# Start offsets of split fp32 operands in a one-core transformer stack: from 64- or 128-byte offsets to 1024-byte ones

## The chip, the cores and the metric

The program runs on one core of a Trainium2 chip, in one launch. The metric is the device time of that launch in microseconds. Three runs of the kernel before took 2493.84, 2503.16 and 2496.09 us; the median is 2496.09 us.

## The reference, cut to what matters

The model works on 256 tokens of width 1024 in float32. A first block has a mixer (gated delta rule and mLSTM side by side), a gated feed-forward part of 22 x 128 hidden units and a small gated embedding. A second block has a linear recurrence (RG-LRU), a PEER layer, forgetting attention, and another PEER layer. A PEER layer scores 16,384 experts per token through 8 heads with 2 x 128 sub-keys and combines the 16 best of each head:

```python
h = _rmsnorm(x, g_ffn)
x = x + (jax.nn.silu(h @ w1) * (h @ w3)) @ w2
...
q = (xc @ q_w).reshape(TOKEN_CHUNK, PEER_HEADS, 2, PEER_HALF)
u = jnp.take(expert_u, expert, axis=0)
act = jax.nn.gelu(jnp.einsum('thkd,td->thk', u, xc).astype(jnp.float32), approximate=False)
w = (g * act).astype(xc.dtype)
return jnp.einsum('thk,thkd->td', w, jnp.take(expert_v, expert, axis=0))
```

Nearly all of the arithmetic is products of a 256-token activation with a weight of 1024 rows or columns. The kernel computes both PEER products densely, over all 16,384 experts, and multiplies by a gate that is zero for the experts that were not chosen.

## The kernel before, in words

**Split products.** Every large float32 product is made of three passes in the type fp32r. An operand x is split into `hi` (x rounded to fp32r, a ScalarE copy) and `lo` (x minus hi, on VectorE or GpSimd); the product is hi*hi + hi*lo + lo*hi, all summed in one PSUM bank (`mm3`; its matmuls carry line L323).

**Weights** come as 766 blocks of 128 x 1024 floats (512 KB) through one queue of loads on SyncE, in the order of use (`Stream`). Each block passes through three tiles: `raw` (4 buffers, L202), `whi` (2 buffers, cast at L209) and `wlo` (2 buffers, subtracted at L257 on VectorE or L259 on GpSimd). `sub_pattern` says block by block which of the two engines subtracts.

**Activations** stand feature-major in SBUF: `hh` and `hl` are the two halves of the normalized activation, [128 partitions, 8 slices of features, 256 tokens], so a slice is 1024 bytes in each partition. Other split operands have their own tiles: `oab` (both mixer outputs), `fh`/`fl` (the feed-forward's hidden slice), `p` (the embedding), `xbh`/`xbl` (the recurrence), `rawh`/`rawl` (the activation before its norm is known: the product is made on unscaled rows and scaled after, `norm`, `set_raw` and `linear`; with a shift column these rows hold 258 values, 1032 bytes).

**Which operand moves.** A matmul loads a 128 x 128 stationary operand (a weight load, PEld in the profile) and streams the moving one through it. In `block`/`mm3` (L323) and `kblock` (L1051) the weights are stationary and 256 tokens move: 256 columns, 1024 bytes. In `tblock` (L1065, the PEER v stage), and in `alin` and attention's values, 128 tokens are stationary and 512 columns of `whi` or `wlo` move: 2048 bytes.

**Stages on the time line**: mixer 0 to 262 us, feed-forward to 459, embedding to 490, recurrence to 652, PEER queries and selection to 800, PEER u to 1126, PEER v to 1482 (its last 8 blocks by `kblock`), attention to 1652, and the second PEER layer to the end (u from about 1800, v from 2137). In the u stage, eight tokens at a time, VectorE builds one-hot tiles `ohB`, `ohE` and `ohA` in 16-bit types (L1583 to L1591) and TensorE multiplies them to the gate `G` (L1600), between the weight blocks.

**Where tiles lie.** The allocator gives each tile the next free multiple of 32 bytes in a partition; 16384 bytes at the bottom are reserved as a DMA scratch. With this the built kernel before has these starts, as bytes past a multiple of 1024:

| tile | role | before |
|---|---|---|
| hh, hl | moving (L323, L1051); stationary (L1065) | 128 |
| whi, wlo | stationary (L323, L1051); moving (L1065) | 448 |
| oab, p | moving (L323) | 448 |
| fh, fl | moving (L1051) | 768 |
| xbh, xbl; rawh, rawl of the embedding | moving | 704 |
| rawh, rawl of 258 columns | moving | 448 to 600, each slice 8 bytes on from the last |
| ohB, ohA | stationary and moving of G | 448 |
| raw | written by the load | 448 |

Of the kernel before, what the change touches and what calls it, by code (L numbers as in the profile page):

```python
# [8 lines left out]
F32 = mybir.dt.float32  # L9
FR = mybir.dt.float32r  # L10
BF = mybir.dt.bfloat16
# [6 lines left out]
P = 128  # L18
# [4 lines left out]
NR = 11  # L23
EPS = 1e-6
BIG = 1e30
TB = 8
TAIL = 8
NLATE = 3
# [153 lines left out]
class Stream:  # L182
# [16 lines left out]
    def _ahead(self, b, n, loads, his, los):  # L199
        while self.nl < min(n, loads) or self.nh < min(n, his) or self.ns < min(n, los):  # L200
            if self.nl < min(n, loads) and self.nl < self.ns + b.raw_bufs:
                t = b.spool.tile([P, D], F32, name="raw", tag="raw", bufs=b.raw_bufs)[:, :self.width(self.nl)]  # L202
                self.load = b.nc.sync.dma_start(t, self.seq[self.nl])
                self.raw[self.nl] = t
                self.nl += 1
                continue
            if self.nh < min(n, his) and self.nh < self.nl:
                t = b.spool.tile([P, D], FR, name="whi", tag="whi", bufs=b.hi_bufs)[:, :self.width(self.nh)]
                b.nc.scalar.copy(t, self.raw[self.nh])  # L209
                self.hi[self.nh] = t  # L210
                self.nh += 1
                continue
            if self.ns < self.nh:
                i = self.ns
                t = b.spool.tile([P, D], FR, name="wlo", tag="wlo", bufs=b.lo_bufs)[:, :self.width(i)]
                b.sub(t, self.raw.pop(i), self.hi[i].bitcast(F32), i)
                self.lo[i] = t
                self.ns += 1
                continue
            raise AssertionError  # L220
# [9 lines left out]
class Build:  # L230
# [121 lines left out]
    def setup(self):  # L352
        nc, pp, d = self.nc, self.pp, self.d
        self.xT = pp.tile([P, KC, S], F32, name="xT")
        self.hh = pp.tile([P, KC, S], FR, name="hh")
        self.hl = pp.tile([P, KC, S], FR, name="hl")
        with self.tc.high_priority(offset=5000):
            for k in range(0, KC, 2):
                nc.sync.dma_start(self.xT[:, k:k + 2], d["xT"][:, k:k + 2])
        self.cst = pp.tile([P, N_PERSIST, P], F32, name="cst")  # L360
        self.cols = pp.tile([P, N_COLS], F32, name="cols")
        nc.scalar.dma_start(self.cols, d["cols"])
        nc.scalar.dma_start(self.cst, d["const"][:, :N_PERSIST])
        self.ident = self.cst[:, C_ID]
        self.ones = self.cst[:, C_ONE]
        self.mhalf = pp.tile([P, 1], F32, name="mhalf")
        nc.vector.memset(self.mhalf, -0.5)
        self.lam = self.colr("lam")
        self.mods = [pp.tile([P, 24], F32, name=f"mod{i}") for i in range(4)]
        self.gsc = [pp.tile([P, KC], F32, name=f"gsc{i}") for i in range(4)]  # L370

        order = []

        def add(k, lo=0, hi=None):
            n = d[k].shape[0]
            order.extend(d[k][i] for i in range(lo, n if hi is None else hi))

        add("w_in")
        add("w_ba")
        add("w_bb")  # L380
        add("w_out")
        for j in range(NFF):
            add("w1", j, j + 1)
            add("w3", j, j + 1)
            if j:
                add("w2", j - 1, j)
        add("w2", NFF - 1, NFF)
        add("w_ple")
        add("w_pg")
        for j in range(NR + GLAG):  # L390
            if j < NR:
                add("l_in", j, j + 1)
            if j >= GLAG:
                i = j - GLAG
                order.append(d["l_gate"][i][:, :2 * len(PAIRS[i]) * P])
        add("l_in", NR, 2 * NR)
        add("l_out")
        for l in (0, 1):
            if l:
                add("f_in")  # L400
                add("f_out")
            add(f"q{l}")
            add(f"u{l}")
            add(f"v{l}")
        self.ws = Stream(self, order)
# [83 lines left out]
                                            op0=OP.mult, op1=OP.subtract)  # L489

    def raw_tiles(self, pool, wide=True):
        w = S + 2 if wide else S
        return (pool.tile([P, KC, w], FR, name="rawh"), pool.tile([P, KC, w], FR, name="rawl"),
                pool.tile([P, S], F32, name="rawb"),
                lambda: (pool.tile([P, S], F32, name="rawt", bufs=2), pool.tile([P, 1], F32, name="rawc", bufs=2)))

# [78 lines left out]
    def mix(self, mp, scr):  # L575
# [2 lines left out]
        gab = mp.tile([P, 16, S], F32, name="gab")  # L578
        gz = mp.tile([P, H, S], F32, name="gz")
        mo = mp.tile([P, H, S], F32, name="mo")  # L580
        oab = mp.tile([P, 16, S], FR, name="oab")
        self.oab = [oab[:, 4 * i:4 * i + 4] for i in range(4)]
        self.norm(scr, self.colr("g_mix"), raw=(
            oab[:, 0:8], oab[:, 8:16], gab[:, 0], lambda: (gab[:, 1 + self.nraw % 2], None)))
# [487 lines left out]
    def ffn(self, fp, scr, fin):  # L1072
# [7 lines left out]
        for j in range(NFF + 1):  # L1080
            if j < NFF:
                p1 = self.linear(self.mmt())
                p3 = self.linear(self.aux("p3"))
                s = fp.tile([P, S], F32, name="fs", bufs=2)
                nc.scalar.activation(s, p1, AF.Silu)
                nc.vector.tensor_tensor(s, s, p3, op=OP.mult)
                h = fp.tile([P, S], FR, name="fh", bufs=3)
                l = fp.tile([P, S], FR, name="fl", bufs=3)
                self.split(h, l, s)
                hm[j] = (h, l)  # L1090
            if j:
# [2 lines left out]
            if j == 8:  # L1094
                pT = fin.tile([P, 2, S], F32, name="pT")
                nc.scalar.dma_start(pT, self.d["pT"])
                self.p_split = [fin.tile([P, 2, S], FR, name=f"p{i}") for i in range(2)]
                for k in range(2):
                    self.split(self.p_split[0][:, k], self.p_split[1][:, k], pT[:, k])
        for n in range(KC):  # L1100
# [76 lines left out]
    def lru(self, fin, scr):  # L1177
        nc = self.nc
        with ExitStack() as es:
            lp = es.enter_context(self.tc.tile_pool(name="lru", bufs=1))  # L1180
            xb = lp.tile([P, NR, S], F32, name="xb")
            xh = lp.tile([P, NR, S], FR, name="xbh")
            xl = lp.tile([P, NR, S], FR, name="xbl")
            hs = lp.tile([P, NR, S], F32, name="hs")
            lam = self.lam
            self.phase("lru")
# [237 lines left out]
    def peer(self, l):  # L1424
# [4 lines left out]
        with ExitStack() as es:  # L1429
# [4 lines left out]
            def region(kb, size):  # L1434
# [3 lines left out]
            es1 = es.enter_context(ExitStack())  # L1438
            rp = es1.enter_context(self.tc.tile_pool(name="raw", bufs=1))
            self.phase(f"peer{l}")  # L1440
            self.norm(big[:, 112:128], self.gsc[mi], self.mods[mi][:, 0:8], raw=(
                rp.tile([P, KC, S + 2], FR, name="rawh"), rp.tile([P, KC, S + 2], FR, name="rawl"), big[:, 0],
                lambda: (big[:, 1 + self.nraw % 2], flat[:, 3 * S + self.nraw:3 * S + self.nraw + 1])))
            qT = region(0, 4096).rearrange("p (a b) -> p a b", a=16)
            sk = region(16, 2048).rearrange("p (a b) -> p a b", a=16)
# [125 lines left out]
            def spread():  # L1571
# [8 lines left out]

                for t0 in range(0, S, TB):
                    tq = slice(t0, t0 + TB)
                    B = op.tile([P, H, P, 2], BF, name="ohB", bufs=2)  # L1583
                    nc.vector.tensor_tensor(B, iop, pairs(items[:, 1, tq]), op=OP.is_equal)
                    nc.vector.tensor_tensor(B, B, pairs(items[:, 2, tq]), op=OP.mult)
                    yield
                    E = op.tile([P, H, P, 2], HF, name="ohE", bufs=1)
                    nc.vector.tensor_tensor(E, iop, pairs(items[:, 0, tq]), op=OP.is_equal)
                    A = op.tile([P, 2, H, P, 2], HF, name="ohA", bufs=2)
                    for i in range(2):  # L1590
                        nc.vector.tensor_tensor(A[:, i], E, pairs(sig[:, i, tq]), op=OP.mult)  # L1591
                    yield
# [148 lines left out]
```

## Time and profile before

| | |
|---|---|
| profiled execution | 2497.24 us |
| its span, first to last instruction | 2495.4 us |
| median of three runs | 2496.09 us |
| TensorE busy | 2380.4 us, 95%, 17450 matmuls |
| weight loads | 2226.6 us, 89% |
| VectorE busy | 1923.4 us, 77% |
| ScalarE busy | 1256.8 us, 50% |
| GpSimd busy | 716.1 us, 29% |
| mean granted TensorE clock | 0.985 |
| data moved | 460 MB, mean 184 GB/s |

A reader should know three things of this profile. The matmuls are pipelined and their ends are modelled: a row's duration (say 1.11 us for 8 matmuls) is longer than the distance to the next row, so the cost of one matmul is read from the distance between the starts of consecutive rows, divided by the count. TensorE works at one of two levels, 1.2 and 2.4 GHz; a granted clock of 1.00 is the upper one. And a VectorE instruction that is held up by GpSimd counts as busy while it is held up.

### The profile page before, as it was taken

The page shows a single profiled execution, that of the slowest core. Times are in us where ns is not written, and L with a number is a line of the kernel's source. Part 1 is how long each engine was busy: PE and PEld are TensorE (multiplying, and loading weights), DVE is VectorE, ACT ScalarE, POOL GpSimd, SP SyncE. Part 2 cuts the span into 40 slices and gives each one's busy share as a digit, 9 for nine tenths or more (in the row PEclk, how much of TensorE's full clock was granted, in tenths as well). Part 3 has the DMA queues.
Part 4 walks back from the last instruction along what each step waited for, and adds up shares of the span by engine and source line. Part 5 has one row for each costly group of instructions (what it writes and reads, how often), then busy time and mean ns, then how long its engine had stood idle before and what let it go on. Part 6 is the DMA issues. An engine that isn't in the chain of part 4 may idle for free. (4 is left out here: it accounts for less than half of the span.)

```text
span 2495.4 us, 44808 instructions
## 1 busy us (share of the span) xinstructions
PE 2380.4 (95%) x17450; PEld 2226.6 (89%) x17450; DVE 1923.4 (77%) x3481; ACT 1256.8 (50%) x2229; POOL 716.1 (29%) x361
## 2 busy tenths in 40 slices
PE   8989999987998999999999998899799999999999
PEld 8989999887998999997888898789799999888888
DVE  7585866889598999986666668878979998655555
ACT  7644544665553444445444556555344444444444
POOL 4635300355666323330000026246522222000000
PEclk9999999989998999999999999999899999999999
DMA  5475677434554555557777755555455555566654
GB/s 192 154 242 190 208 250 251 165 115 137 168 170 139 166 169 161 171 166 245 238 237 244 223 173 192 203 176 161 127 170 161 173 167 169 186 194 191 190 193 152
DMA packets 127252, 460.26 MB, mean 184 GB/s; under 512 B 14128, under 2 KB 14784, under 8 KB 126784
## 3 DMA queue, kind: packets, MB, share of 16 engines
q1 hardware_dynamic: 126000, 454.55, 56.2%
q8 instruction: 136, 2.23, 0.4%
q10 hardware_dynamic: 1040, 2.86, 0.3%
q14 instruction: 76, 0.62, 0.1%
HBM read 456.29 MB, written 1.05 MB: 183 GB/s over the span
## 5 line engine op out<-in xcount | busy, mean ns | idle before, releaser
L209 ACT CAST whi<-raw 128x1024 fp32r<-128x1024 f32 (+1 forms) x766 | 800.8, 1046 | 1000.5 <-PE acc L1065 325.9
L257 DVE TENSOR_TENSOR wlo<-raw,whi 128x1024 fp32r<-128x1024 f32 (+1 forms) x551 | 694.2, 1260 | 378.9 <-ACT whi L209 363.9
L259 POOL TENSOR_TENSOR wlo<-raw,whi 128x1024 fp32r<-128x1024 f32 (+2 forms) x215 | 566.7, 2641 | 754.0 <-ACT whi L209 440.4
L1065 PE MATMUL acc<-whi,hh 128*128 128x512 f32 x960 | 260.5, 392 | 2.6 <-ACT whi L209 1.1
L323 PE MATMUL mm<-hh,whi 128*128 128x256 f32 x1704 | 247.5, 286 | 15.7 <-ACT whi L209 6.6
L1065 PE MATMUL acc<-whi,hl 128*128 128x512 f32 x960 | 259.4, 391 | 0.0
L1065 PE MATMUL acc<-wlo,hh 128*128 128x512 f32 x960 | 259.1, 392 | 0.0
L323 PE MATMUL mm<-hh,wlo 128*128 128x256 f32 x1704 | 245.1, 286 | 13.6 <-DVE wlo L257 11.2
L323 PE MATMUL mm<-hl,whi 128*128 128x256 f32 x1704 | 246.1, 284 | 5.8 <-POOL hl L531 2.9
L323 PEld LDWEIGHTS mm<-hh,whi 128*128 128x128 f32 x1704 | 219.6, 191 | 20.1 <-ACT whi L209 7.8
L323 PEld LDWEIGHTS mm<-hh,wlo 128*128 128x128 f32 x1704 | 219.6, 192 | 16.2 <-DVE wlo L257 12.4
L323 PEld LDWEIGHTS mm<-hl,whi 128*128 128x128 f32 x1704 | 220.5, 192 | 8.3 <-POOL hl L531 4.0
L323 PE MATMUL acc<-hh,wlo 128*128 128x256 f32 x1464 | 207.6, 286 | 14.8 <-DVE wlo L257 12.0
L1065 PEld LDWEIGHTS acc<-whi,hh 128*128 128x128 f32 x960 | 180.1, 188 | 43.1 <-ACT whi L209 1.6
L1065 PEld LDWEIGHTS acc<-whi,hl 128*128 128x128 f32 x960 | 180.3, 188 | 39.8
L1065 PEld LDWEIGHTS acc<-wlo,hh 128*128 128x128 f32 x960 | 180.3, 188 | 39.3
L323 PE MATMUL acc<-hh,whi 128*128 128x256 f32 x1464 | 210.0, 286 | 0.1
L323 PE MATMUL acc<-hl,whi 128*128 128x256 f32 x1464 | 204.6, 281 | 0.0
L323 PEld LDWEIGHTS acc<-hh,wlo 128*128 128x128 f32 x1464 | 189.9, 194 | 15.8 <-DVE wlo L257 12.6
L323 PEld LDWEIGHTS acc<-hh,whi 128*128 128x128 f32 x1464 | 187.4, 192 | 0.3 <-ACT whi L209 0.3
L323 PEld LDWEIGHTS acc<-hl,whi 128*128 128x128 f32 x1464 | 186.4, 190 | 0.0
L422 DVE SCALAR_TENSOR_TENSOR modw<-modw,cb 128x1024 f32<-128x1024 f32 x96 | 130.7, 1366 | 21.5 <-DMA modw<-in_mod_dram 15.2
(523 smaller groups left out, 3304.1 us busy)
## 6 DMA issues: line engine op xcount, KB each, us to landing
raw<-in_u_dram SPq DMA_DIRECT2D x256, 512.0 KB, 3.7
raw<-in_v_dram SPq DMA_DIRECT2D x256, 512.0 KB, 4.1
modw<-in_mod_dram SPq DMA_DIRECT2D x96, 512.0 KB, 4.7
raw<-in_w_dram SPq DMA_DIRECT2D x66, 512.0 KB, 4.3
raw<-in_w_in_dram SPq DMA_DIRECT2D x45, 512.0 KB, 4.2
raw<-in_f_in_dram SPq DMA_DIRECT2D x33, 512.0 KB, 3.6
raw<-in_q_dram SPq DMA_DIRECT2D x32, 512.0 KB, 3.6
raw<-in_l_in_dram SPq DMA_DIRECT2D x22, 512.0 KB, 3.5
```

The source lines that it names most:

```text
L209: b.nc.scalar.copy(t, self.raw[self.nh])
L257: self.anchor = self.nc.vector.tensor_tensor(out, a, b, op=OP.subtract)
L259: self.nc.gpsimd.tensor_tensor(out, a, b, op=OP.subtract)
L323: self.last_mm = mm(ps, t[a], t[b], start=(i == 0), stop=(i == n - 1))
L422: self.later(nc.vector.scalar_tensor_tensor(t, t, 1.0, cb, op0=OP.mult, op1=OP.mult, accum_out=self.mods[i][:, j:j + 1]))
L1065: self.last_mm = mm(accs[h][tb], x[:, tb * P:(tb + 1) * P], w[:, h * 512:(h + 1) * 512], start=(first and i == 0), stop=(last and i == 2))
```

## The change

Every tile that is an operand of a split product gets a start at a multiple of 1024 bytes: `raw`, `whi`, `wlo`, `hh`, `hl`, `oab`, `fh`, `fl`, `p`, `xbh`, `xbl`, `rawh`, `rawl`. The 258-column rows of `rawh`/`rawl` are laid 288 floats (1152 bytes) apart where they were 258 floats (1032 bytes) apart. The three one-hot tiles start at multiples of 256 bytes. The DMA scratch at the bottom of SBUF shrinks from 16384 to 1024 bytes, which makes room for the gaps.

```diff
+ROW = 1024
+RAWW = 288
...
-                t = b.spool.tile([P, D], F32, name="raw", tag="raw", bufs=b.raw_bufs)[:, :self.width(self.nl)]
+                t = b.spool.tile([P, D], F32, name="raw", tag="raw", align_bytes=ROW, bufs=b.raw_bufs)[:, :self.width(self.nl)]
...
-                t = b.spool.tile([P, D], FR, name="whi", tag="whi", bufs=b.hi_bufs)[:, :self.width(self.nh)]
+                t = b.spool.tile([P, D], FR, name="whi", tag="whi", align_bytes=ROW, bufs=b.hi_bufs)[:, :self.width(self.nh)]
...
-                t = b.spool.tile([P, D], FR, name="wlo", tag="wlo", bufs=b.lo_bufs)[:, :self.width(i)]
+                t = b.spool.tile([P, D], FR, name="wlo", tag="wlo", align_bytes=ROW, bufs=b.lo_bufs)[:, :self.width(i)]
...
-        self.hh = pp.tile([P, KC, S], FR, name="hh")
-        self.hl = pp.tile([P, KC, S], FR, name="hl")
+        self.hh = pp.tile([P, KC, S], FR, name="hh", align_bytes=ROW)
+        self.hl = pp.tile([P, KC, S], FR, name="hl", align_bytes=ROW)
...
-        w = S + 2 if wide else S
-        return (pool.tile([P, KC, w], FR, name="rawh"), pool.tile([P, KC, w], FR, name="rawl"),
+        w, n = (RAWW, S + 2) if wide else (S, S)
+        h, l = (pool.tile([P, KC, w], FR, name=k, align_bytes=ROW)[:, :, :n] for k in ("rawh", "rawl"))
+        return (h, l,
...
-        oab = mp.tile([P, 16, S], FR, name="oab")
+        oab = mp.tile([P, 16, S], FR, name="oab", align_bytes=ROW)
...
-                h = fp.tile([P, S], FR, name="fh", bufs=3)
-                l = fp.tile([P, S], FR, name="fl", bufs=3)
+                h = fp.tile([P, S], FR, name="fh", bufs=3, align_bytes=ROW)
+                l = fp.tile([P, S], FR, name="fl", bufs=3, align_bytes=ROW)
...
-            xh = lp.tile([P, NR, S], FR, name="xbh")
-            xl = lp.tile([P, NR, S], FR, name="xbl")
+            xh = lp.tile([P, NR, S], FR, name="xbh", align_bytes=ROW)
+            xl = lp.tile([P, NR, S], FR, name="xbl", align_bytes=ROW)
...
-                    B = op.tile([P, H, P, 2], BF, name="ohB", bufs=2)
+                    B = op.tile([P, H, P, 2], BF, name="ohB", bufs=2, align_bytes=256)
...
-    nc = _bacc.Bacc("TRN2", target_bir_lowering=False, num_devices=1)
+    nc = _bacc.Bacc("TRN2", target_bir_lowering=False, num_devices=1, dynamic_dma_scratch_size=1024)
```

No instruction is moved, added or removed: built, the two kernels have the same instructions in the same order on all five engines, each waiting on the same semaphores. Only addresses differ. In the changed kernel `hh`, `hl`, `whi`, `wlo`, `raw`, `oab`, `p`, `fh`, `fl`, `xbh`, `xbl` and the 256-column `rawh`/`rawl` all start at 0 past a multiple of 1024; slice k of a 258-column row starts at 128 x k past one; a 128-column weight slice starts at 0 or 512; `ohB` starts at 512 and `ohA` at 768. Tiles that the change does not name (`xT`, `scr`, `big`, `gab`, `cst` and the rest) lie 2 to 15 KB lower, at other offsets of 32 bytes.

## Rows read from the trace of the kernel before

**Rows 1.** The page's first parts: engines, and the span in 40 slices.
```profile
span 2495.4 us, 44808 instructions
PE 2380.4 (95%) x17450; PEld 2226.6 (89%) x17450; DVE 1923.4 (77%) x3481; ACT 1256.8 (50%) x2229; POOL 716.1 (29%) x361
...
PEclk9999999989998999999999999999899999999999
```
**Rows 2.** Busy time by stage: engine busy us (instructions), granted clock, DMA share, GB/s.
```profile
0.00:290.00 290.00, 265.11 (x2123) 258.54 (x2124) 212.61 (x356) 168.21 (x296) 146.54 (x85) 0.98 0.56 194
290.00:445.00 155.00, 155.00 (x1318) 155.00 (x1317) 98.14 (x129) 70.37 (x92) 0.00 (x0) 1.00 0.74 249
445.00:655.00 210.00, 181.45 (x1400) 175.81 (x1399) 172.51 (x252) 128.19 (x243) 110.53 (x80) 0.93 0.43 144
655.00:800.00 145.00, 130.01 (x1059) 127.83 (x1058) 129.23 (x476) 70.51 (x118) 93.84 (x37) 0.96 0.46 147
800.00:1130.00 330.00, 328.08 (x3008) 324.63 (x3008) 306.08 (x452) 146.35 (x306) 104.74 (x34) 1.00 0.53 169
1130.00:1482.00 352.00, 350.85 (x1637) 291.75 (x1636) 229.17 (x316) 176.12 (x262) 7.78 (x5) 1.00 0.72 231
1482.00:1665.00 183.00, 166.31 (x1250) 152.51 (x1250) 145.72 (x322) 109.47 (x246) 82.06 (x50) 0.99 0.57 191
1665.00:1800.00 135.00, 115.92 (x957) 114.41 (x957) 121.52 (x457) 65.98 (x107) 79.77 (x36) 0.95 0.45 141
1800.00:2137.00 337.00, 334.64 (x3069) 332.48 (x3068) 304.33 (x456) 149.43 (x312) 90.84 (x37) 0.99 0.53 168
2137.00:2490.00 353.00, 352.77 (x1645) 293.56 (x1645) 201.93 (x267) 172.18 (x256) 0.00 (x0) 1.00 0.59 185
```
**Rows 3.** PE in order of time, feed-forward: start us, us, what, count.
```profile
300.03 1.11 PE L1051 MATMUL acc<-fh,whi 128*128 128x256 f32 x8
...
304.74 1.10 PE L323 MATMUL mm<-hh,wlo 128*128 128x256 f32 x8
```
**Rows 4.** PE in order of time, mixer.
```profile
55.12 1.07 PE L323 MATMUL mm<-hh,wlo 128*128 128x256 f32 x8
...
58.75 1.07 PE L323 MATMUL acc<-hh,whi 128*128 128x256 f32 x8
```
**Rows 5.** PE in order of time, recurrence's output product.
```profile
641.52 1.12 PE L1051 MATMUL acc<-xbh,wlo 128*128 128x256 f32 x8
...
644.40 1.12 PE L1051 MATMUL acc<-xbh,wlo 128*128 128x256 f32 x8
```
**Rows 6.** PE in order of time, attention's products on 258 columns.
```profile
1493.95 1.12 PE L323 MATMUL mm<-rawl,whi 128*128 128x258 f32 x8
1494.91 1.15 PE L323 MATMUL acc<-rawh,whi 128*128 128x258 f32 x8
1495.90 1.12 PE L323 MATMUL acc<-rawl,whi 128*128 128x258 f32 x8
```
**Rows 7.** PE in order of time, PEER v.
```profile
1200.26 1.08 PE L1065 MATMUL acc<-whi,hh 128*128 128x512 f32 x4
...
1203.01 1.08 PE L1065 MATMUL acc<-whi,hh 128*128 128x512 f32 x4
```
**Rows 8.** PE in order of time, mLSTM: plain fp32 products, two records each.
```profile
117.49 0.59 PE L1021 MATMUL mnum<-scr,mv 128*128 128x256 f32 x2
117.92 0.38 PE L1022 MATMUL mnum<-scr,mv 128*128 128x128 f32 x2
```
**Rows 9.** PE in order of time, last blocks of PEER v.
```profile
1458.94 0.62 PE L1051 MATMUL aux<-hh,whi 128*128 128x256 f32 x4
...
1462.11 0.62 PE L1051 MATMUL mm<-hl,whi 128*128 128x256 f32 x4
```
**Rows 10.** The one-hot line L1585 on VectorE: durations ns, min/median/max.
```profile
L1585 DVE TENSOR_TENSOR ohB<-ohB,items x64: 674/679/2903, 787.8 to 2100.8; 128x1024 bf16<-128x1024 bf16 x64
```
**Rows 11.** Chain that ended last, by piece: start us, us, what.
```profile
2137.39 329.19 PE acc L1065 x1437
```

More of the change, by code (lines that the diff above doesn't have):

```diff
@@ L1096, in ffn @@
                 nc.scalar.dma_start(pT, self.d["pT"])
-                self.p_split = [fin.tile([P, 2, S], FR, name=f"p{i}") for i in range(2)]
+                self.p_split = [fin.tile([P, 2, S], FR, name=f"p{i}", align_bytes=ROW) for i in range(2)]
                 for k in range(2):
@@ L1440, in peer @@
             self.phase(f"peer{l}")
+            rh, rl = (rp.tile([P, KC, RAWW], FR, name=n, align_bytes=ROW)[:, :, :S + 2] for n in ("rawh", "rawl"))
             self.norm(big[:, 112:128], self.gsc[mi], self.mods[mi][:, 0:8], raw=(
-                rp.tile([P, KC, S + 2], FR, name="rawh"), rp.tile([P, KC, S + 2], FR, name="rawl"), big[:, 0],
+                rh, rl, big[:, 0],
                 lambda: (big[:, 1 + self.nraw % 2], flat[:, 3 * S + self.nraw:3 * S + self.nraw + 1])))
@@ L1586, in spread @@
                     yield
-                    E = op.tile([P, H, P, 2], HF, name="ohE", bufs=1)
+                    E = op.tile([P, H, P, 2], HF, name="ohE", bufs=1, align_bytes=256)
                     nc.vector.tensor_tensor(E, iop, pairs(items[:, 0, tq]), op=OP.is_equal)
-                    A = op.tile([P, 2, H, P, 2], HF, name="ohA", bufs=2)
+                    A = op.tile([P, 2, H, P, 2], HF, name="ohA", bufs=2, align_bytes=256)
                     for i in range(2):
```

## The prediction

> **What bounds the kernel now.** I read the page's first parts first, then the busy time by stage, then single rows of TensorE in order of time. The reader is to see that TensorE is busy for 95% of the span and that its granted clock is near 1 in nearly all slices [rows 1], the upper level, 2.4 GHz, so the time is the number of matmuls times the cost of one, plus the stretches where something else is waited for. The stages divide it [rows 2]. Five of them have TensorE busy for over 99%: feed-forward (155 us), u (330 and 337 us), v (352 and 353 us), together 1527 us. In the other five (963 us) it is busy for 859, and chains of the mixers, the recurrence, the selection and attention end last in between. The chain that ended last is one unbroken run of 1437 wide matmuls [rows 11]: nothing but their own rate sets the second v stage.
>
> So the change, which moves no instruction and alters only start offsets, can act only through the rate of one instruction, and that rate is worth looking at. Distances between starts, divided by the count, give for 256 columns: 4.71 us for 40 matmuls, 117.8 ns, with moving operands 768 and 128 bytes past a multiple of 1024 [rows 3]; 3.63 us for 32, 113.4 ns, with 128 past [rows 4]; 2.88 us for 24, 120.0 ns, with 704 past [rows 5]. For 258 columns at scattered offsets two sets of eight take 1.95 us, 121.9 ns each [rows 6]. For 512 columns at 448 past it is 2.75 us for 12, 229.2 ns [rows 7]. At 2.4 GHz one column per cycle would be 106.7 and 213.3 ns. A bound from a row: a plain fp32 product streams 256 columns in two records 0.43 us apart, 215 ns each [rows 8], which is 512 cycles and little more. It takes two cycles a column, so it asks for bytes at half the rate, and at that rate an offset of 448 costs nothing that shows. The split products pay 6% to 12% over their columns, and the amount goes with the offset: 704 and 448 are 64 past a multiple of 128, and 768 and 128 are not.
>
> A reading that fits: at full rate the moving stream is fetched in lines of 128 bytes, 32 columns, 13.3 ns each. A row of 1024 bytes that begins 64 past touches nine lines: 120.0 ns, as measured. One of 1032 bytes touches nine wherever it begins: 121.9. One of 2048 bytes that begins 64 past touches seventeen: 226.7 of the 229.2. A row on a line boundary touches eight: 106.7, and the 113.4 or 117.8 measured leave 7 to 11 ns for something else. Two things could be it that the change also touches: the weight slices, which begin 64 past a line and so touch five lines for four, and the row's crossing of a multiple of 1024.
>
> **The change part by part.** *Stationary and moving operands at 1024.* The trace has no matmul at full rate with both operands on a boundary, so the cost is bounded from both sides. Below: 107.5 ns for 256 columns and 215 for 512 (half of, and all of, the fp32 row [rows 8]). Above: each keeps the worst that 256 columns show, 120.0 [rows 5], and 512 columns grow by 6.6 ns, the step between 113.4 and 120.0, to 235.8. I take 110 and 218, near the low end, since 1024-byte rows then touch the fewest lines and cross nothing, but not at it, since no row at full rate shows an overhead under 6 ns for 256 columns.
>
> The sum, by stage. Feed-forward: 1318 matmuls [rows 2] x (117.8 - 110) = 10.3 us. The u stages: 6077 instructions [rows 2], of which 1024 are the gate products on 16-bit tiles, leaves some 5050 x 7.8 = 39.4 us. The v stages: 2880 wide ones (two layers of 1440; the chain's run has 1437 of one [rows 11]) x (229.2 - 218) = 32.3 us, and 384 narrow ones at the end, which already run at 3.17 us for 28, 113.2 [rows 9], x 3.2 = 1.2 us. The other stages: some 5,100 matmuls of 256 or 258 columns (11,874 and 384 in the program less those above), at between 113.4 and 121.9, mean saving near 6: 31 us, of which I count half, 15 us, because TensorE waits there for 104 of 963 us [rows 2] and what it gains before such a wait is lost in it.
>
> In u the cover has to be examined. VectorE is busy for 306 and 304 us there [rows 2], so it is late next. But some of this is held-up time: L1585 takes 674 ns at least and 2903 at most [rows 10], 2.2 us more when GpSimd's subtraction is running. Its own work leaves room, though not everywhere; I count four fifths, 31.5 us. In v the wider load is on the transfers: 231 GB/s at a share of 0.72 [rows 2] becomes 5% more, below the 249 that the feed-forward stage moves; that stage itself would go to some 267, at a share of 0.8. I take both as hidden.
>
> *258-column rows 1152 bytes apart.* 384 matmuls, on a line boundary but still nine lines: between 0 and 8 ns each, at most 3 us, within the last term.
>
> *One-hot tiles at 256.* VectorE's 679 ns [rows 10] has no offset in the trace to compare it with; the same line starts at 448 in all 64 cases. I take nothing, with bounds of 10% of 64 x 0.68 us, 4 us either way.
>
> *raw at 1024, smaller scratch, other tiles moved.* The loads land whole kilobytes either way, and no DMA is issued from GpSimd in either kernel; nothing, within 3 us.
>
> Sum: 10.3 + 31.5 + 32.3 + 1.2 + 15 = 90 us off the profiled execution's 2497.2 (span 2495.4 and 1.8 around it), which stands 1.1 us over the median. Forecast: 2407 us.
>
> **The rivals.** *Only the best seen.* Every narrow matmul comes to 113.4 and every wide one to 226.7, because the last 6 ns are no matter of offsets. For it: no row at full rate is under 113, and 113 occurs with no line to spare. Then feed-forward gives 1318 x 4.4 = 5.8, u 5050 x 4.4 = 22.2, v 2880 x 2.5 = 7.2, the rest some 10 x 0.6 = 6: 41 us, 2456 us.
>
> *Nothing.* The offsets mean nothing and 113, 118 and 120 are three ways in which the pipeline happens to lock. For it: 113.4 and 117.8 occur with the same operands at the same offsets [rows 3, 4]. Against it: 120.0 goes with 64 past. The time would be 2490 to 2503.
> [...]
>
> *Slower: both streams in step.* The weight load of the next matmul runs beside the moving stream. Before, 128 against 448 puts the two 64 past each other, modulo 128; where both are 64 past, they are in step, and this is where 120.0 is seen [rows 5]. If the collision is between the streams, then the change puts all of them in step. From the first block on, narrow matmuls go to 120.0 and wide ones to 235.8: 1318 x 2.2 + 5050 x 2.2 + 2880 x 6.6 + 384 x 6.8 = 36 us, and 10 in the other stages: 2543 us. Against it: it leaves unexplained why the wide ones, out of step, are 16 ns over their columns.
>
> **How the numbers follow.** Near the low bound (2375 to 2435): 0.38. Only the best seen (2435 to 2475): 0.23. Nothing (2485 to 2505): 0.15. In step, in whole or in part (2510 to 2560): 0.24. What a measurement of this kernel can tell from no change is about 0.5%, 12 us. Faster by more than that 0.61, within it 0.15, slower 0.24. The lowest time that the bounds give is 1318 x 10.3 + 5050 x 10.3 + 2880 x 14.2 + 384 x 5.7 = 109, and 20 elsewhere: 2368 us. The range that leaves out about 2 in 10 runs from 2372 to 2520; the likeliest case's own is 2375 to 2435.
>
> **What would show it.** Right: in the feed-forward stage eight narrow matmuls take 0.88 us and not 0.94, in v four wide ones 0.87 and not 0.92, with weight loads, casts and subtractions as long as before, and the chain that ended last is still the run of L1065. The five other stages shorten by less than their matmuls do. If narrow ones are at 113 everywhere the first rival holds; if they are at 120, or the wide ones above 0.93 for four, the streams' relation decides and not the boundary. Wrong in another way: matmuls at 110 but a u stage as long as before, with VectorE at 99% and its wait for GpSimd unchanged.

## The result, and the profile after

The changed kernel takes 2509.66 us (median of 7 runs, 2508.85 to 2516.76) against 2494.75 us (7 runs, 2489.91 to 2503.16) for the kernel before: ratio 1.0063, 95% interval 1.0051 to 1.0075. It is slower by 0.6%; forecast were 2407 us and a gain.

The page's first parts after, which answer to [rows 1]: the same counts of instructions, the same granted clock, 24 us more of TensorE.

```profile
span 2510.1 us, 44808 instructions
PE 2404.7 (96%) x17450; PEld 2257.9 (90%) x17450; DVE 1930.8 (77%) x3481; ACT 1259.6 (50%) x2229; POOL 709.4 (28%) x361
...
PEclk9999999989999999999999999999899999999999
```

Busy time by stage after, in four of the stretches of [rows 2] (the columns are the same):

```profile
290.00:445.00 155.00, 155.00 (x1293) 155.00 (x1293) 98.27 (x129) 69.52 (x91) 0.00 (x0) 1.00 0.74 243
...
800.00:1130.00 330.00, 325.12 (x2938) 323.14 (x2937) 304.82 (x445) 141.71 (x296) 98.92 (x34) 0.99 0.52 163
1130.00:1482.00 352.00, 349.57 (x1626) 292.08 (x1626) 229.77 (x312) 179.43 (x267) 2.41 (x1) 1.00 0.71 232
...
1800.00:2137.00 337.00, 333.41 (x3018) 331.66 (x3018) 312.88 (x459) 145.65 (x301) 92.90 (x38) 0.99 0.53 165
```

In the feed-forward stretch TensorE is busy all the time at a granted clock of 1.00 in both kernels, and gets through 1293 matmuls where it got through 1318: each one costs more. Single rows of TensorE after, in order of time (start us, us, what, count), with mixer, feed-forward, recurrence, v and its last blocks:

```profile
55.27 1.12 PE L325 MATMUL mm<-hh,wlo 128*128 128x256 f32 x8
...
59.11 1.12 PE L325 MATMUL acc<-hh,whi 128*128 128x256 f32 x8
...
303.31 1.12 PE L1054 MATMUL acc<-fh,whi 128*128 128x256 f32 x8
...
308.11 1.12 PE L325 MATMUL mm<-hh,wlo 128*128 128x256 f32 x8
...
646.39 1.12 PE L1054 MATMUL acc<-xbh,whi 128*128 128x256 f32 x8
...
649.27 1.12 PE L1054 MATMUL acc<-xbh,whi 128*128 128x256 f32 x8
...
1200.48 1.07 PE L1068 MATMUL acc<-wlo,hh 128*128 128x512 f32 x4
...
1203.20 1.07 PE L1068 MATMUL acc<-wlo,hh 128*128 128x512 f32 x4
...
1470.04 0.64 PE L1054 MATMUL mm<-hl,whi 128*128 128x256 f32 x4
...
1473.40 0.64 PE L1054 MATMUL aux<-hl,whi 128*128 128x256 f32 x4
```

Read as before, by the distance of the starts (*narrow* matmuls have 256 columns, *wide* ones 512): the mixer's 32 narrow matmuls take 3.84 us, 120.0 ns each, where [rows 4] had 113.4; the feed-forward's 40 take 4.80, 120.0, for 117.8 [rows 3]; the recurrence's 24 take 2.88, 120.0, as before [rows 5]; the 28 at the end of v take 3.36, 120.0, for 113.2 [rows 9]. Over the whole program the narrow ones average 119.8 ns: they have come to the slowest steady pace that the kernel before showed at this width at a granted clock of 1.00. The wide ones went the other way: 12 in 2.72 us, 226.7 ns, for 229.2 [rows 7]. The chain that ended last has the same long piece, shortened from 329.19 us [rows 11] to

```profile
2154.33 326.01 PE acc L1068 x1437
```

By stage, between starts of matmuls that mark the stages (u: first gate product to first wide matmul; v: first to last wide one), with the mean distance between the starts of neighbouring narrow (256) or wide (512) matmuls, in ns; two versions of the experiments beside them:

| stage | before: us, ns | after: us, ns | e1: us, ns | e9: us, ns |
|---|---|---|---|---|
| mixer | 283.6, 116.1 | 286.7, 119.8 | 281.7, 114.6 | 287.2, 114.5 |
| feed-forward | 175.6, 117.8 | 178.7, 120.0 | 169.2, 113.5 | 169.0, 113.4 |
| embedding to selection | 350.5, 116.4 | 353.8, 119.8 | 351.1, 114.7 | 353.4, 114.4 |
| u, first layer | 317.0, 117.6 | 320.5, 119.9 | 315.1, 115.9 | 313.5, 114.2 |
| v, first layer (wide) | 331.5, 228.9 | 329.1, 226.7 | 330.1, 228.9 | 328.3, 226.7 |
| end of v to selection | 363.1, 115.0 | 364.5, 119.7 | 362.5, 114.8 | 361.1, 114.6 |
| u, second layer | 314.9, 117.7 | 319.8, 119.9 | 309.6, 115.5 | 305.7, 114.0 |
| v, second layer (wide) | 330.0, 228.9 | 326.8, 226.7 | 330.0, 228.9 | 326.8, 226.7 |
| to the last matmul | 23.8, 114.2 | 24.8, 119.7 | 23.8, 114.0 | 24.0, 114.8 |

The differences of the stages, after less before, add up to 14.7 us, which is the difference of the spans (2510.1 and 2495.4). Each column is one execution; a second one of the kernel before (e10 below) differs from the first by up to 1.3 us in a stage, so a single difference of about 1 us says little. In e9 the first and the third stage are no shorter than before although their narrow matmuls are 1.6 and 2.0 ns faster.

### The profile page after: what moved, and what is told of

It reads as the page before. It is cut to its first block, busy times and chain, and to the rows that moved or that the text cites. A ratio compares the mean times of both kernels' runs of the same rounds, so it can differ in the third digit from the quotient of the medians.

```text
span 2510.1 us, 44808 instructions
## 1 busy us (share of the span) xinstructions
PE 2404.7 (96%) x17450; PEld 2257.9 (90%) x17450; DVE 1930.8 (77%) x3481; ACT 1259.6 (50%) x2229; POOL 709.4 (28%) x361
## 3 DMA queue, kind: packets, MB, share of 16 engines
q10 hardware_dynamic: 1040, 2.86, 0.3%
## 5 line engine op out<-in xcount | busy, mean ns | idle before, releaser
L259 DVE TENSOR_TENSOR wlo<-raw,whi 128x1024 fp32r<-128x1024 f32 (+1 forms) x551 | 687.8, 1248 | 381.5 <-ACT whi L211 363.8
L261 POOL TENSOR_TENSOR wlo<-raw,whi 128x1024 fp32r<-128x1024 f32 (+2 forms) x215 | 560.5, 2612 | 773.7 <-ACT whi L211 486.7
L325 PE MATMUL mm<-hh,whi 128*128 128x256 f32 x1704 | 253.2, 289 | 15.3 <-ACT whi L211 6.0
L325 PE MATMUL mm<-hl,whi 128*128 128x256 f32 x1704 | 253.2, 288 | 5.5 <-POOL hl L534 2.7
L325 PEld LDWEIGHTS mm<-hl,whi 128*128 128x128 f32 x1704 | 227.7, 196 | 7.8 <-POOL hl L534 3.8
L325 PE MATMUL acc<-hh,whi 128*128 128x256 f32 x1464 | 213.2, 288 | 0.0
```

Source lines behind the costliest of these rows:

```text
L259: self.anchor = self.nc.vector.tensor_tensor(out, a, b, op=OP.subtract)
L261: self.nc.gpsimd.tensor_tensor(out, a, b, op=OP.subtract)
L325: self.last_mm = mm(ps, t[a], t[b], start=(i == 0), stop=(i == n - 1))
```

## The experiments

In what follows, the *distance* of a matmul is the start of its moving operand less the start of its stationary one, in bytes in a partition, modulo 256. Before: `hh`, `hl` to `whi`, `wlo` 128 - 448, that is 192; `fh`, `fl` 64; `oab`, `p`, `xbh`, `xbl` 0; the wide ones 448 - 128, that is 64. After: 0 everywhere.

**e1 and e2: one operand moved by 64 bytes.** Both are the changed kernel with a helper that begins a tile some floats past the boundary; e1 moves only `whi` and `wlo`, e2 only the token operands.

```diff
+def shifted(pool, shape, by, **kw):
+    n = int(np.prod(shape[1:]))
+    t = pool.tile([P, n + by], FR, align_bytes=ROW, **kw)[:, by:by + n]
...
-        self.hh = pp.tile([P, KC, S], FR, name="hh", align_bytes=ROW)
+        self.hh = shifted(pp, [P, KC, S], SM, name="hh")
...
-                t = b.spool.tile([P, D], FR, name="whi", tag="whi", align_bytes=ROW, bufs=b.hi_bufs)[:, :self.width(self.nh)]
+                t = shifted(b.spool, [P, D], SW, name="whi", tag="whi", bufs=b.hi_bufs)[:, :self.width(self.nh)]
```

e1 has `SM, SW = 0, 16`, e2 `SM, SW = 16, 0`.

> The changed kernel with one thing undone: whi and wlo start 64 bytes past their multiple of 1024; all other operands stay at 0. Theory A (the rate hangs on the distance between the moving row and the weight slice, modulo 128): narrow products go back to the two old paces, 113.3 and 117.8 ns, the wide ones from 226.7 back to 228.9; the time is that of before, 2490 to 2500 us, or up to 5 us less, since the 978 narrow ones on oab, p, xbh, xbl and the embedding's rows leave 120.0 too. Rival B (something else in the change costs the 15 us: the smaller scratch, the moved tiles, the 1152-byte rows): narrow ones may go back, but the time stays at 2505 to 2515.

> The mirror of the last: whi and wlo at 0, every token operand (hh, hl, oab, p, fh, fl, xbh, xbl, rawh, rawl) 64 bytes past its multiple of 1024. Theory A (only the distance modulo 128 counts): again 113.3 or 117.8 ns for narrow products, 228.9 for wide ones, 2485 to 2500 us. Rival C (absolute starts count: the moving row has to begin on a line of 128 bytes, the weight slice off it, as in the kernel before): narrow products, whose moving rows now begin 64 past a line, stay at 120.0 or go above; 2505 to 2520 us.

e1 took 2482.37 us (6 runs) against 2492.30 before: ratio 0.9964 (0.9950 to 0.9978). Sixty-four bytes in `whi` and `wlo` alone turn a loss of 0.6% into a gain of 0.4%. e2 took 2508.41 us (6 runs), ratio 1.0063 (1.0046 to 1.0081), as slow as the changed kernel, although its operands are as far apart as e1's. e1 came out 3 us below its expected range, and e2 outside the 2485 to 2500 of theory A. Rows of TensorE in e1, feed-forward and u (same columns):

```profile
300.29 1.07 PE L333 MATMUL mm<-hh,whi 128*128 128x256 f32 x8
...
303.01 1.07 PE L333 MATMUL p<-hh,whi 128*128 128x256 f32 x8
...
822.57 1.11 PE L333 MATMUL acc<-hl,whi 128*128 128x256 f32 x8
...
829.16 1.10 PE L333 MATMUL mm<-hh,wlo 128*128 128x256 f32 x8
830.11 1.09 PE L1612 MATMUL G<-ohA,ohB 128*128 128x128 f16 x16
...
832.01 1.07 PE L333 MATMUL acc<-hl,whi 128*128 128x256 f32 x8
...
838.36 1.07 PE L333 MATMUL mm<-hh,wlo 128*128 128x256 f32 x8
```

In the feed-forward part 24 narrow matmuls take 2.72 us: 113.3 ns. In u there are two paces with the same operands: 56 in 6.59 us, 117.7, up to the gate products, and 56 in 6.35 us, 113.4, behind them. And in e2's v stage 12 wide matmuls take 2.80 us, 233.3 ns each:

```profile
1200.46 1.10 PE L1076 MATMUL acc<-wlo,hh 128*128 128x512 f32 x4
...
1203.26 1.10 PE L1076 MATMUL acc<-wlo,hh 128*128 128x512 f32 x4
```

Over the whole program e1's narrow matmuls average 114.9 ns and its wide ones 228.9; e2's 117.6 and 233.3. So +64 and -64 are not alike, which a distance modulo 128 would make them. Modulo 256 they are 64 and 192, and then the four kernels agree: narrow 120 at 0, 117.7 at 64, 113.3 or 117.8 at 192; wide 226.7 at 0, 228.9 at 64, 233.3 at 192. Against the changed kernel e2's narrow matmuls gain 2.2 ns each, which rival C rules out, and its wide ones lose 6.5, which takes most of it back: that its time lies in rival C's range is chance.

**e3 and e4: benches of the pace alone.** A kernel without the model, which runs rows of 32 narrow or 16 wide matmuls at chosen starts, behind small gaps of other matmuls, four times each.

```diff
+            for rep in (64, 96, 128, 160):
+                for m, s in NARROW:
+                    gap(rep)
+                    run(f"n{m}w{s}a", 256, narrow(m, s, 8))
+                    ps = run(f"n{m}w{s}b", 256, narrow(m, s, 32))
```

> No part of the model: on one core, runs of 8 and 32 narrow matmuls (256 columns) and of 4 and 16 wide ones (512) with nothing to wait for, at 20 and 9 pairs of offsets, each four times after a plain fp32 product of 64, 96, 128 or 160 columns; the output is filled with the input. Theory A: narrow pairs with a distance of 0 modulo 128 (0/0, 64/64, 128/0, 256/0, 448/448) at 120.0 ns, whatever their absolute start; distances of 64 at 113.3 or 117.8 by the run that comes before; other distances in between or better. Wide: 226.7 at distance 0, 228.9 at 64. Rival C (absolute starts): 0/0 and 64/64 differ, and 64/0 differs from 0/64. If no pair is under 113.3 and 226.7, the floor of the prediction (107.5 and 215) does not exist for full-rate products.

> The model is left out; the output is the input, copied. Rows of 32 matmuls of 256 columns and of 16 of 512 columns follow each other without a wait, at every distance (moving start less stationary start) of 16 bytes from 0 to 240, at some distances with both starts moved together, and with stationary operands of 64 and 32 columns. Theory D (the distance modulo 256 alone sets the pace, since the moving stream and the weight load of the next matmul meet in the same banks): distances 0, 256 and equal starts give 120.0 ns for 256 columns wherever both begin, 64 gives 117.8, 192 gives 113.3 (117.8 in some rows), and (0,64), (64,128), (128,192) are alike; 512 columns give 226.7 to 227.4 at 0, 228.9 at 64, 233.4 at 192; with a stationary operand of 64 or 32 columns the differences shrink, as the weight load reads less. Rival C (the absolute start of the moving row in a line of 128 bytes decides, the weight slice little): (0,64), (64,128) and (128,192) differ by 3 ns or more, and (448,0) is unlike (192,0). Rival N (what ran before the row decides, not the offsets): the four repeats of one pair, behind four kinds of gap, differ as much as different pairs do.

Four rows of e3; the name gives the starts (n, moving, w, stationary), and a row lasts 31 distances and the 0.28 us of its last matmul:

```profile
299.57 4.00 PE L48 MATMUL n0w0b<-X,W 128*128 128x256 f32 x32
...
344.16 3.79 PE L48 MATMUL n192w0b<-X,W 128*128 128x256 f32 x32
...
358.98 4.00 PE L48 MATMUL n64w64b<-X,W 128*128 128x256 f32 x32
...
363.98 3.94 PE L48 MATMUL n0w64b<-X,W 128*128 128x256 f32 x32
```

That is 120.0, 113.2, 120.0 and 118.1 by this arithmetic; by the starts 120.0, 113.35, 120.0 and 117.8 (this last pair took 113.3 in its three other rows). The mean distances between starts in e4, ns, stationary operand at 0 (two values where the repeats split two and two):

```
moving at       0     16     32     48     64     80     96    112
narrow      120.0  118.7  117.0  118.3  117.8  119.7  120.0  113.5
wide        227.6  231.8  233.4  233.3  228.9  231.1  233.5  231.1 (226.6 once)
moving at     128    144    160          176          192          208    224    240
narrow      119.1  118.6  117.7        119.2  113.3/117.8        119.1  118.3  117.1
wide        232.4  233.3  234.2  231.1/233.3        233.4  230.1/234.6  233.2  235.5
```

Pairs with both starts moved together, (64,128), (128,192), (32,96) and (0,64), all at distance 192, take 113.3 or 117.8 like (192,0), as do (448,0), (704,0) and (0,320); (64,64), (32,32) and (448,448) take 120.0 in e3. So for the multiples of 32 tried the distance decides and the place does not, except that at 192 two paces are possible. Below that it is not the whole rule: (16,160) is at distance 112 and takes 113.5, but (0,144), at the same distance, 118.5 to 120.0. At multiples of 8 that are none of 16 four pairs were tried, and none is fast: (104,0) takes 122.5 (120.0 once), (120,0) and (200,0) 120.8 to 121.8, (184,0) 120.0. No pair is under 113.3.

The last part of e4 makes the weight load smaller. With half of it, the stationary operand has 64 columns (h, moving, w, stationary, k).

```profile
259.27 3.79 PE L57 MATMUL h0w0k64b<-X,W 128*64 128x256 f32 x32
...
273.89 3.97 PE L57 MATMUL h192w0k64b<-X,W 128*64 128x256 f32 x32
```

Now distance 0 takes 113.3 (four of four rows) and 192 takes 119.0: the order of the two is turned round with the same moving rows. The pace depends on what the weight load reads, not on the moving stream alone. With 32 stationary columns distance 0 takes 120.0, 117.8, 117.7 and 113.3 in its four rows and 192 takes 113.3 to 113.4 (116.7 once), so there is no simple trend with the width. That the differences would shrink was wrong. Why the relation of the two counts, by a meeting in banks as e4's theory has it or otherwise, no run shows.

**e5 and e6: the place, and the rest of the change.** e5 is `SM, SW = 16, 16` with the helper's tiles at multiples of 256, so all is in step again but nothing begins on a line of 128 bytes. e6 keeps all else of the change and gives the operands their old distances (the raw rows `rawh`, `rawl`, some 5% of the narrow matmuls, are not put back):

```diff
-SM, SW = 0, 0
+SM, SW = 32, 48
...
-        oab = shifted(mp, [P, 16, S], SM, name="oab")
+        oab = shifted(mp, [P, 16, S], SW, name="oab")
...
-                h = shifted(fp, [P, S], SM, name="fh", bufs=3)
+                h = shifted(fp, [P, S], 0, name="fh", bufs=3)
```

> Moving and stationary operands both begin 64 bytes past a multiple of 256, so no 256-column row begins on a line of 128 bytes and all are at distance 0; all else as in the changed kernel. Theory D: narrow 120.0, wide 226.8, the time of the changed kernel, 2500 to 2515 us. Rival C (start of the row on a line decides): narrow rows 64 past a line with weight slices 64 past behave unlike those at 0, wide ones at 229 to 233, and the time leaves the changed kernel's by 10 us or more. Rival P (the slowness of the changed kernel comes from something else that it moved, such as raw, the one-hot tiles or the smaller scratch): the same as theory D, so this run does not separate it.

> All of the change stays (raw at 1024, one-hot tiles at 256, 1152-byte rows, small scratch, nothing of the operands where it was), but every operand gets the distance modulo 256 that it had before: hh, hl to whi, wlo 192, fh, fl 64, oab, p, xbh, xbl 0. Theory D: narrow in the mixture of 113.3 and 117.8 as before, wide 228.9, and the time of the kernel before, 2488 to 2500 us. Rival P (the other moved tiles cost the 15 us): 2505 us or more though the matmuls are as before. Rival C: narrow near 120, 2500 us or more, since absolute starts are none of before's.

e5: 2508.81 us, ratio 1.0045 (1.0028 to 1.0061), narrow 119.9, wide 226.8: the changed kernel again. Its feed-forward rows, 32 in 3.84 us:

```profile
300.05 1.12 PE L333 MATMUL p<-hh,wlo 128*128 128x256 f32 x8
...
303.89 1.12 PE L333 MATMUL mm<-hh,whi 128*128 128x256 f32 x8
```

e6: 2489.06 us (10 runs), ratio 0.9972 (0.9960 to 0.9984): the loss is gone with the distances, so `raw`, the one-hot tiles and the small scratch can't be what cost 15 us. It is even 8 us under the kernel before: its narrow matmuls at distance 192 average 114.4, against 116.5: more of its rows fall into the faster of the two paces, in u nearly all (113.7 and 113.6). The second u stage is 9.8 us shorter for it (305.1 us). The first gives nothing back (317.0 us, as before); TensorE's waits there (engine, line, waited for: us in total, times, longest) show where most of it went:

```profile
PE mm L333 <- POOL wlo L269: 6.9, 10, 2.3
```

The subtraction on GpSimd is late next; the kernel before lost 1.1 us to it in the same stage. Because the paces changed too, e6 does not show that the rest of the change is free to the microsecond.

**e7, e8 and e9: a version with both paces at their best.** Narrow matmuls want distance 192 or 112, wide ones 0, but the same `hh` and `whi` serve both, with the roles exchanged. e7 is e1 with tiles of their own for the v stage's tokens, at distance 0; e8 has the same, and 112 for the narrow ones (`SM, SW = 28, 0`, rows of 258 columns 1280 bytes apart); e9 is e8 with these tiles allocated at the start of the PEER layer (in e9 alone 30 wide matmuls at the start of the first v stage also stand in another order).

```diff
+            vp = es.enter_context(self.tc.tile_pool(name="vtok", bufs=1))
+            vh, vl = (shifted(vp, [P, 4, S], SW, name=k) for k in ("vh", "vl"))
...
-                self.split(self.hh[:, e % 4], self.hl[:, e % 4], big[:, e])
+                self.split(*slot(e), big[:, e])
```

> e1 with one thing more: the stationary token rows of the v stage's wide products get tiles of their own, 64 bytes past a multiple of 256 like whi and wlo, so distance 0 for 2880 wide matmuls, while narrow ones keep distance 192. Theory D: wide ones go from 228.9 to 226.8, 2880 x 2.1 = 6.0 us off, from 2482 to some 2476, and narrow ones stay at 114.9 in the mean. Rival T (the transfers, not the matmuls, set the v stage): its two stages stay at 330.2 and 330.0 us and the time at 2482.

> whi and wlo at 0 past a multiple of 256, all moving token operands 112 past one (rows of 258 columns 1280 bytes apart), and the v stage's own stationary tiles at 0: narrow distance 112, wide distance 0. Theory D with the bench's numbers: narrow 113.3 to 113.9 in all rows, without the slower state of 117.8, against a mean of 114.9 in e1: 11,150 x 1.4 = 16 us of TensorE, of which some 56% reached the end so far (27 us of a difference of 49 between e1 and the changed kernel), 9 us, and 6 us from the wide ones: some 2467 us, faster than all so far. Rival L (the bench's pace at 112 holds only behind the gaps it used, and the kernel's own breaks put it into other states, 117 to 120): a narrow mean over 115.5 and a time of 2477 us or more.

> e8 with the v stage's own stationary tiles in the PEER layer's long-lived pool, so that their first split waits for no memory that the u stage gives back. Theory H (the 3 us of faster wide products were lost in e7 and e8 to a wait for the first split at the start of v): no wait of 3.6 us for vh, the first v stage 327.3 us or less (329.9 and 328.2 in e7 and e8), the time 2 to 4 us under e8, 2477. Rival: that wait hides under something as late, and the time stays at 2480 or above.

e7: 2483.58 us, ratio 0.9961 (0.9946 to 0.9977), no better than e1 and not the expected 2476, though its wide matmuls do come to 226.7. A layer's saving, 1440 x 2.2 ns = 3.2 us, is lost at the start of its v stage, where TensorE now waits for the first split (e1: 0.54 us):

```profile
PE acc L1076 <- ACT vh L350: 3.6, 1, 3.6
```

The tile takes memory that the u stage gives back late. And the wait costs more than its 3.6 us. Busy time and, behind the five engines, the granted clock, in the last 4 us of u, the wait, the first 3.7 us of v, and a little later:

```profile
1113.00:1117.00 4.00, 4.00 (x38) 4.00 (x37) 2.58 (x4) 1.51 (x3) 0.00 (x0) 1.00 0.73 213
1117.50:1121.20 3.70, 0.19 (x2) 0.00 (x0) 2.90 (x6) 2.23 (x8) 0.00 (x0) 1.00 0.64 192
1121.30:1125.00 3.70, 3.70 (x9) 2.90 (x10) 1.41 (x4) 2.15 (x4) 0.00 (x0) 0.55 0.72 234
1126.00:1128.00 2.00, 2.00 (x10) 1.67 (x9) 0.00 (x0) 0.00 (x0) 0.00 (x0) 1.00 0.77 307
```

TensorE was idle for 3.6 us at a granted clock of 1.00 and came back at 0.55 in the mean of the next 3.7 us: nine matmuls, most at 430 ns for 227. Eight such distances are 1.6 us more. Wait and clock together take 3.1 + 1.6 = 4.7 us where 3.2 were saved; 1.7 us more go to a wait for a cast of `whi` soon after. The second layer has the same wait of 3.6 us.

e8: 2480.63 us, ratio 0.9939 (0.9926 to 0.9952), not the expected 2467; narrow 114.2 in the mean, and the same wait of 3.6 us. Rows of its u stage, the second to the ninth set of eight behind the gate products:

```profile
809.17 1.09 PE L333 MATMUL acc<-hl,whi 128*128 128x256 f32 x8
810.09 1.07 PE L333 MATMUL acc<-hh,wlo 128*128 128x256 f32 x8
...
815.53 1.07 PE L333 MATMUL mm<-hh,wlo 128*128 128x256 f32 x8
```

The eight ahead of these, right behind the break, take longer still; the second eight take 0.92 us, 115.0 each, and then 48 take 5.44 us, 113.3. So e8's rows settle at the faster pace some 16 matmuls behind a break, where at distance 192 a row can keep 117.8 to its end (e1).

e9: 2474.25 us (5 runs), ratio 0.9910 (0.9894 to 0.9927), the wait gone. Its first v stage, 328.3 us, missed the expected 327.3, with 1.5 us of waits for casts of `whi`; the gain over e8 lies mostly in the u stages (313.5 and 305.7 us for 317.3 and 309.0), at whose end the wait stood. It is the fastest version here, 0.9% under the kernel before. Its rows in the feed-forward stage, and the longest piece of its last chain:

```profile
300.18 1.07 PE L333 MATMUL p<-hh,whi 128*128 128x256 f32 x8
...
302.90 1.07 PE L1062 MATMUL acc<-fh,whi 128*128 128x256 f32 x8
```

```profile
2124.06 321.26 PE acc L1076 x1416
```

**e10: the kernel before, once more.** No edit.

> The kernel before, once more, for the paces of its narrow matmuls. Theory R (at distance 192 two paces exist, 113.3 and 117.8, and which one a row falls into is set anew at each break by timing): the mean of the narrow ones at distance 192 comes out elsewhere between 113.5 and 117.5 in some stage, and the time moves with it. Rival (the build fixes it): 116.5 in the mean again, 117.6 and 117.7 in the two u stages, as in the profiled execution before.

One run of 2496.47 us. Narrow matmuls at distance 192 average 116.5 again, and the two u stages 117.7 and 117.7. Which of the two paces a row takes is set again at a break (e1 above), but in these two executions it comes out nearly the same (the mixer's mean moves from 116.1 to 115.7): the rival was right. That e6, another build with the same distances for these operands, differs by 2 ns is then likely a matter of the build. What in it picks the pace stays open.

**e11: other types.** The bench with bfloat16 and plain float32 operands.

> The model is left out; the output is the input, copied. Rows of 32 matmuls as in the benches before, now with both operands in bfloat16 (256 and 512 columns) and in plain float32 (256 columns, two records each), at eight pairs of starts in bytes, and two fp32r pairs for reference (0,0) and (192,0). Theory D2 (the meeting of the moving stream and the weight load costs only where the two together ask for 4-byte operands at one column a cycle): bfloat16, which asks for half the bytes, takes one pace for all pairs within 1%, and so does plain float32 (two cycles a column); fp32r shows 120.0 and 113.3 or 117.8 again. Rival D3 (the relation of the starts costs TensorE in every type): bfloat16 and float32 differ between pairs by 2% or more.

Rows named by type (r fp32r, h bfloat16), columns, m moving, w stationary:

```profile
24.12 3.66 PE L54 MATMUL h256m0w0b<-XB,WB 128*128 128x256 bf16 x32
...
102.12 3.66 PE L54 MATMUL h256m192w0b<-XB,WB 128*128 128x256 bf16 x32
...
267.28 4.00 PE L54 MATMUL r256m0w0b<-X,W 128*128 128x256 f32 x32
272.56 3.79 PE L54 MATMUL r256m192w0b<-X,W 128*128 128x256 f32 x32
```

By the starts, bfloat16 takes 109.2 ns for 256 columns and 215.8 for 512 at all eight pairs, without exception, and plain float32 215.8 for each of its two records. Of the three types only fp32r depends on the starts in these rows (120.0 and 113.3).

## Why the prediction was wrong

**What bounds the kernel: right.** What the trace shows to change is the pace of a matmul; the clock and all counts stayed, and the chain that ended last is the same run of wide products.

**The step that failed: "at full rate the moving stream is fetched in lines of 128 bytes", and from it 110 and 218 ns for operands on a boundary.** It explained 120.0 by a moving row that touches nine lines [rows 5]. After the change every row of 256 columns touches eight and still takes 120.0 where the sum had 110, and wide ones take 226.7 where it had 218; in e5 all of 256 columns touch nine and nothing differs. What the 120.0 of [rows 5] had in common with the changed kernel was the relation of two starts: `xbh` at 704 and `wlo` at 448 are 256 apart, distance 0. The prediction looked at one operand's offset where the traced rows held both, and 704 - 448 could have been worked out from the table of starts. Its own sign for this was met: narrow ones at 120 were to mean that the relation of the two streams decides and not the boundary.

**The bound from the fp32 row** (107.5 and 215) was a bound that fp32r never came near. What a column takes, which the prediction puts at 106.7 ns for 256, the runs show as a pace: e11's bfloat16 rows take 106.6 ns for 256 columns more (215.8 less 109.2) at a granted clock of 0.999 in the mean of the run, 2.40 columns a nanosecond. At 0.50, the only value beside 1.00 that the granted clock has in the traces of before and after, the kernel before takes 1.71 us for eight matmuls of 256 columns, 213.8 ns each (213.3 by the starts) or 1.20 columns a nanosecond:

```profile
43.80 1.91 PE L323 MATMUL mm<-hh,wlo 128*128 128x256 f32 x8
45.51 1.03 PE L323 MATMUL mm<-hl,whi 128*128 128x256 f32 x4
...
43.00:46.00 3.00, 3.00 (x17) 3.00 (x16) 2.48 (x5) 2.94 (x6) 0.00 (x0) 0.50 0.05 16
```

Read as one column per cycle, these are the 2.4 and 1.2 GHz of the two levels; no trace gives the clock itself in GHz. e11 also confirms the fp32 row itself, 215.8 at every pair, but the means of fp32r rows never went under 113.3 and 226.6, one sixteenth over their columns (106.6 and 213.2). That fp32 is spared because it asks for bytes at half the rate, no run shows. The excess of wide products, which the prediction counted as lines to be saved, is mostly this floor.

**The rivals.** "Slower: both streams in step" had the direction, the relation of the two streams as what decides, and for narrow matmuls the price, 120.0. Weight loads do run beside the moving stream: in the trace before, the eight of one set start at 1029.98 us and its matmuls at 1030.09, behind those of the set ahead, which stream from 1029.09 on. This rival's modulus of 128 was wrong (e1 and e2 are both 64 out of step and differ). So was its wide price: 235.8 supposed, 226.7 measured, since wide products are fastest at distance 0. With that term corrected its 2543 us become 2543 - 2880 x 9.1 ns = 2517, and 2510 came. That the stated range, 2372 to 2520, holds the 2510 is owed to this rival alone: forecast and sign were wrong. The argument held against it, that wide ones out of step are 16 ns over their columns, is answered by the floor (13.3 of the 16). "Only the best seen" had the right floor, 113.4 and 226.7, and the wrong place for it. "Nothing", three ways in which the pipeline locks, is half true: at distance 192 two paces exist side by side, but 120.0 goes with distance 0. That the offsets mean nothing holds in e11 for bfloat16 (109.2 and 215.8 at all eight pairs) and float32 (215.8), and not for fp32r, where the stationary operand's start and width change the pace of the same moving rows (113.3 to 120.0).

**The sum by stage.** Pairs of neighbouring matmuls times the differences of the table: narrow +4.9 us in the mixer, +3.3 feed-forward, +6.3 embedding to selection, +5.3 and +5.0 in the u stages, +7.9 from the end of v to the second selection, +1.0 at the end, wide -6.3: 27.4 us (some 30 with the matmuls beside breaks counted too). Measured 14.7. Where TensorE is hardly idle (feed-forward, u, v and the end) 8.3 give 6.9; in the other stages 19.1 give 7.8, 41%. The prediction's half for these stages was a fair measure, with the sign turned. Its four fifths for a gain in u fit e1 and e9: for the 2400 narrow matmuls that each of these stages has between its marks, e1 kept 7.2 of 9.4 us and e9 12.7 of 17.0, but e6 only 9.8 of 19.2. What TensorE then waits for in the first layer is the subtraction on GpSimd (2.3, 4.7 and 6.9 us in e1, e9 and e6), where the prediction looked at VectorE. Its count of the other stages was 384 short (11,874 and 384 less the rest leave 5,506), which is 1 us of its forecast.

**Costs put at nothing.** The one-hot line after, which answers to [rows 10] (min, median and max in ns):

```profile
L1589 DVE TENSOR_TENSOR ohB<-ohB,items x64: 674/679/2908, 796.1 to 2117.1; 128x1024 bf16<-128x1024 bf16 x64
```

Unchanged, as supposed. Its long rows end with GpSimd: in the trace before 25 of the 64 take 2884 to 2903 ns, all counted as busy, and each of them begins inside a subtraction on GpSimd (L259) and ends 0.54 to 0.56 us behind its end; five others that begin inside one take 674 to 679 ns. One of the 25, and its subtraction:

```profile
947.10 2.89 DVE L1585 TENSOR_TENSOR ohB<-ohB,items 128x1024 bf16<-128x1024 bf16 x1
...
946.50 2.94 POOL L259 TENSOR_TENSOR wlo<-raw,whi 128x1024 fp32r<-128x1024 f32 x1 [6.55 <-ACT whi L209]
```

For the rest e6 bears the zero out only in the main, as said there.

## What to carry to other kernels

For products of fp32r operands, look at the two starts together: the distance of the moving from the stationary operand modulo 256 bytes moved a 256-column matmul between 113.3 and 120.1 ns here at multiples of 16, and "aligned" (distance 0) was among the slowest for it and the best for 512 columns. Choose it by shape with a small bench before padding tiles; for bfloat16 and float32 none of the eight pairs tried made a difference. An offset by 112 for narrow and 0 for wide products brought this kernel 0.9%. When one number of a trace goes with an offset, ask which other offset it is relative to, and find two rows that share the one and differ in the other.

## What the runs showed of the hardware that was not expected

- At one pair of starts (distance 192) two steady paces exist, 113.3 and 117.8 ns, held for dozens of matmuls until a break (56 at each in e1's u stage); two executions of one build had nearly the same pattern (116.5 in the mean of both). At distance 112 the faster one sets in some 16 matmuls behind a break (e8: eight at 115.0, then 48 at 113.3).
- No fp32r row of any pair tried went under 113.3 ns for 256 columns and 226.6 for 512, where bfloat16 takes 109.2 and 215.8.
- A wait of 3.6 us ahead of e7's v stage was followed by 3.7 us at a granted clock of 0.55; e1's wait of 0.54 us at the same place was followed by 1.00.
- A narrower weight load changes which distance is good: with 64 stationary columns, 0 takes 113.3 and 192 takes 119.0.
